# Inverting the diagonal blocks of a delta rule: two partitions to a block instead of one

## The chip and the metric

One core of one Trainium2 chip runs the whole program. The time is the device time of one launch in microseconds (us), from the first to the last instruction with the launch around it. TensorE multiplies matrices into PSUM, VectorE (DVE) and ScalarE (ACT) move and transform data, GpSimd (POOL) does elementwise work on SBUF, and SyncE (SP) issues most of the transfers. Every engine takes its instructions strictly in its own order, so one that waits holds all that stand behind it.

## The reference

The program is a stack of two small models with 256 tokens of width 1024: a gated FFN, an mLSTM mixer, a second FFN, a gated delta net, a convolutional FFN, a sliding-window attention and a last FFN. The change touches the delta net. Of its 16 heads the part that matters is this, with one lower triangular system to be solved for each chunk:

```python
m = jnp.where(strict, jnp.einsum('bnhcd,bnhsd->bnhcs', k_beta, k) * decay, 0.0)
t_mat = lax.linalg.triangular_solve(m + eye, eye, left_side=True, lower=True,
                                    unit_diagonal=True)
u = jnp.einsum('bnhcs,bnhse->bnhce', t_mat, v_beta)
...
o_i = (jnp.einsum('bhcd,bhde->bhce', qd_i, state)
       + jnp.einsum('bhcs,bhse->bhce', a_i, v_new))
```

The kernel uses chunks of 128 tokens: two chunks for each of the 16 heads, so 32 triangles of 128x128, and each has four 32x32 blocks on its diagonal: 128 blocks to invert.

## The kernel before

All projections are done by `mm3` (lines 247 to 252): a weight tile is split into a high and a low part and multiplied in three matmuls of 128x256, L250, L251 and L252. Such a triple is called a **k-step** below; eight of them make one 128-column projection. In the delta stage 44 such projections (352 k-steps, counted from the fifth projection on) are followed by the output projection `op_all` with 128 k-steps. A weight half (`raw`, eight k-steps) is loaded by SP (L163), cast by ACT to `whi` (L171) and subtracted by DVE to `wlo` (L173), some halves ahead.

Between the k-steps the delta rule itself is woven in. `Weave` keeps a clock of its own with due times for every piece and so decides, when the program is built, where each piece stands among the k-steps on TensorE; at run time the order is fixed. The pieces, for `q8` = 0 to 7 (each holds two heads and so four triangles):

- `stage1` (L930 and on) makes the triangle `u1k`; `ustore` writes it to DRAM (`ud`), and `bload` reads the 32x32 blocks back into `B`, one block on each partition.
- `invert(hf)` runs on POOL for the half `hf` (four `q8`, 64 blocks, 64 partitions): 31 steps of a product (L1016, `tmp`) and an addition (L1021, `Z`), each as long as (31-i)(i+1) elements. Then a copy makes the transpose `Y` (L1022), `X` and `Y` lying interleaved in `Z`, and one DMA writes both to DRAM (L1023, `xyd`). `INVERT_COST` tells the planner's clock how long that takes.
- `levels(q8)` reads its blocks from `xyd` into the diagonal of `XY` with four DMAs on SP's queue (L1047), after the weight load issued last, and joins the blocks to the inverse of the triangle: r32 (L1061), px32 (L1071, L1074), r64 (L1085), px64 (L1090), each followed by a copy on ACT or DVE.
- `solve` and `outp` then apply it: w1, w2, w3 (L1104, L1110, L1118), the output o (L1130 to L1132), a row norm on ACT and DVE, and transposes (L1150) with a gate, after which the head's part of `op_all` may run (mark "h").

These eight chains, called **levels** here, and the transposes of `v` (L815) are all of TensorE's work in the stage beside the k-steps. `XY` has three buffers that are cleared once by POOL at the start (L1000) and are used again; `q8` 6 and 7 take the space of `B` and `Z`, and POOL clears it (L1041, L1044).

The order of the projections is k, half of q, half of z, the rest of q and z, then the 16 of v (`GD_ORDER`). Those of v carry a convolution of three passes on DVE (L746) and a gate (L765).

Of the kernel before, what the change touches and what calls it, by code (L numbers as in the profile page):

```python
# [10 lines left out]
F32 = mybir.dt.float32  # L11
# [27 lines left out]
INVERT_COST = 51.0  # L39
# [81 lines left out]
def stack_kernel(ctx, tc, w, xt, cols, rows, gw, baw, rel, kc, kb, out):  # L121
# [582 lines left out]
    xyd = [gdr.tile([64, 32, 64], F32, name=f"xyd{i}") for i in range(2)]  # L704
# [19 lines left out]
    with tc.tile_pool(name="gd", bufs=1) as gp, tc.tile_pool(name="gw", bufs=2) as gq:  # L724
# [246 lines left out]
        def ustore(q8, j, u):  # L971
            (nc.gpsimd if q8 < 4 else nc.scalar).dma_start(out=urows(4 * q8 + 2 * j), in_=u)
            stored[0] += 1
            if stored[0] % 4 == 0 and stored[0] <= 8:
                bload(stored[0] // 4 - 1)
            if stored[0] == 16:
                yield 0.0, 4.0, 0.0
                bload(2)
                bload(3)
            if stored[0] % 8 == 0:  # L980
                fill.mark("s", stored[0] // 8 - 1)
            yield 0.0, 0.0, 0.0
# [8 lines left out]
        B = gp.tile([128, 32, 32], F32, name="B", tag="B")  # L991
        Z = gp.tile([128, 32, 32, 2], F32, name="Z", tag="Z")
        P_.memset(Z, 0.0)
        P_.memset(Z.rearrange("p a b t -> p (a b t)")[:, 0:2048:66], 1.0)
        tmp = gp.tile([128, 256], F32, name="tmp")

        lastinv = [None]
        xyt = [gp.tile([128, 4, 256], F32, name=f"XY{i}") for i in range(3)]
# [3 lines left out]
        def bload(q):  # L1002
            pr = slice(32 * q, 32 * q + 32)
            (nc.gpsimd if q < 2 else nc.scalar).dma_start(out=B[pr], in_=bass.AP(
                tensor=ud[q // 2].tensor, offset=ud[q // 2].offset + 32 * (q % 2) * 129 * 32,
                ap=[[129 * 32, 32], [128, 32], [1, 32]]))

        def invert(hf):
            p0 = 64 * hf
            pr = slice(p0, p0 + 64)  # L1010
            X, Y = Z[pr, :, :, 0], Z[pr, :, :, 1]
            first = None
            for i in range(31):
                n = 31 - i
                t = tmp[pr, 0:n * (i + 1)].rearrange("p (r j) -> p r j", r=n)
                ins = P_.tensor_tensor(out=t, in0=X[:, i, 0:i + 1].unsqueeze(1).to_broadcast([64, n, i + 1]),  # L1016
                                 in1=B[pr, i, i + 1:32].unsqueeze(2).to_broadcast([64, n, i + 1]), op=ALU.mult)
# [12 lines left out]
        def levels(q8):  # L1030
            u = [unit(), unit()]
            for j in range(2):
                nc.sync.dma_start(out=u[j], in_=urows(4 * q8 + 2 * j))
            t = max(fill.now, turn[0])
            turn[0] = t + 5.0
            yield 0.0, t - fill.now, 0.0
            if q8 < 6:
                XY = xyt[q8 % 3]
            elif q8 == 6:
                XY = gp.tile([128, 4, 256], F32, name="XY", tag="B")  # L1040
                P_.memset(XY, 0.0)  # L1041
            else:
                XY = gp.tile([128, 2048], F32, name="XY", tag="Z")[:, 0:1024].rearrange("p (g c) -> p g c", g=4)
                P_.memset(XY, 0.0)  # L1044
            src = xyd[q8 // 4]
            for a in range(4):
                ins = nc.sync.dma_start(out=XY[32 * a:32 * a + 32, :, 64 * a:64 * a + 64], in_=bass.AP(  # L1047
                    tensor=src.tensor, offset=src.offset + (16 * (q8 % 4) + a) * 2048,
                    ap=[[64, 32], [4 * 2048, 4], [1, 64]]))
                after(lastw[0], ins)  # L1050
            xyv = XY.rearrange("p g (c t) -> p g c t", t=2)
            X, Y = xyv[:, :, :, 0], xyv[:, :, :, 1]
# [12 lines left out]
            for b in (32, 96):  # L1065
                S.copy(r32[b:b + 32], pr[b:b + 32, 0:128].rearrange("p (g n) -> p g n", g=4))
# [9 lines left out]
            for b in (0, 64):  # L1076
                V.tensor_copy(Y[b:b + 32, :, b + 32:b + 64], px[b:b + 32, 0:128].rearrange("p (g n) -> p g n", g=4))
                if b == 0:
                    V.tensor_copy(X[32:64, :, 0:32], px[32:64, 0:128].rearrange("p (g n) -> p g n", g=4))
# [6 lines left out]
            S.copy(r64[64:128], pr[64:128, 0:256].rearrange("p (g n) -> p g n", g=4))  # L1086
# [388 lines left out]
```

## Time and profile before

| | us |
|---|---|
| three runs, lowest, median, highest | 1319.40, 1320.38, 1331.99 |
| the profiled execution | 1322.84 |
| its span | 1321.0 |
| TensorE busy | 1287.4 (97%) |
| DVE, ACT, POOL busy | 942.0 (71%), 787.2 (60%), 129.8 (10%) |

The span is what the trace covers; the 1.84 us around it are launch and end. All times in a trace are counted from the span's start. Matmuls overlap, so a matmul's own duration is longer than its share of the engine: the distance from one start to the next is what counts, and a TensorE busy for 97% may still run well below its rate. `PEclk` is the granted share of TensorE's full clock: 1.00 is 2.4 GHz and 0.50 is 1.2 GHz. A name such as `mm<-XY,u1k` is output, arrow, inputs. The delta stage lies between 541 and 842 us.

### The profile page before, as it was taken

What the parts mean: (1) busy time and instruction counts of PE and PEld (TensorE: products, weight loads), DVE (VectorE), ACT (ScalarE), POOL (GpSimd) and SP (SyncE); (2) the same over time, 40 slices, a digit from 0 to 9 for tenths busy, and PEclk for the clock granted to TensorE, in tenths of its full rate; (3) what the DMA queues carried; (4) which work ended last, traced back from release to release, by engine and by line L of the source; (5) the groups of instructions that cost most, each with busy time, mean ns of one, the idle gap of its engine ahead of it and who ended that gap; (6) DMA issues with size and microseconds to landing.
All of it is one profiled execution on the core that took longest, in us unless ns stands there. A gap on an engine that the chain in (4) does not pass through costs nothing.

```text
span 1321.0 us, 27393 instructions
## 1 busy us (share of the span) xinstructions
PE 1287.4 (97%) x10665; PEld 1250.2 (95%) x10665; DVE 942.0 (71%) x1856; ACT 787.2 (60%) x1823; POOL 129.8 (10%) x196
## 2 busy tenths in 40 slices
PE   9999999999999999999999899999999999999997
PEld 8999999999999999899999888899999989999997
DVE  7866546776777754588887845787886786998851
ACT  6544445665765554466666635766765676777641
POOL 0000000000000000102899200001100000000000
PEclk9999999999999999999999979999999999999998
DMA  7755553543465655226474432368976532476540
GB/s 260 242 175 176 175 176 104 170 146 95 157 201 186 190 182 172 73 92 195 127 229 146 109 124 68 128 172 222 228 219 208 178 97 78 151 236 195 190 158 33
DMA packets 72322, 213.38 MB, mean 162 GB/s; under 512 B 14597, under 2 KB 21285, under 8 KB 72064
## 3 DMA queue, kind: packets, MB, share of 16 engines
q1 hardware_dynamic: 65264, 204.36, 49.1%
q0 software_dynamic: 2240, 5.17, 1.8%
q10 hardware_dynamic: 4688, 2.10, 0.6%
q8 instruction: 84, 1.38, 0.4%
q14 instruction: 46, 0.38, 0.1%
HBM read 207.00 MB, written 4.59 MB: 160 GB/s over the span
## 4 chain that ended last, share of the span: by engine, by line
PE 74%; DVE 11%; DMA 6%; ACT 6%; issue 2%; SPq 0%; DVEq 0%; ACTq 0%
PE mm L250 11%; PE mm L251 11%; PE mm L252 11%; PE st L250 7%; PE st L251 7%; PE st L252 7%; DMA raw<-in_w 6%; DVE wlo L173 4%; ACT whi L171 2%; PE mm L270 2%; PE mm L272 2%; PE mm L268 2%; PE st L268 1%; PE st L272 1%; PE st L270 1%
## 5 line engine op out<-in xcount | busy, mean ns | idle before, releaser
L171 ACT CAST whi<-raw 128x512 fp32r<-128x512 f32 x752 | 439.3, 617 | 320.2 <-PE mm L251 112.4
L173 DVE TENSOR_TENSOR wlo<-raw,whi 128x1024 fp32r<-128x1024 f32 (+1 forms) x377 | 461.5, 1226 | 140.4 <-ACT whi L171 128.7
L250 PE MATMUL mm<-xh,whi 128*128 128x256 f32 (+1 forms) x1040 | 295.2, 284 | 0.1
L252 PE MATMUL mm<-xh,wlo 128*128 128x256 f32 (+1 forms) x1040 | 294.6, 283 | 0.0
L251 PE MATMUL mm<-xl,whi 128*128 128x256 f32 (+1 forms) x1040 | 294.2, 283 | 0.0
L250 PE MATMUL st<-xh,whi 128*128 128x256 f32 (+1 forms) x720 | 206.1, 286 | 1.1 <-DVE u1k L925 1.1
L252 PE MATMUL st<-xh,wlo 128*128 128x256 f32 (+1 forms) x720 | 204.4, 284 | 0.1
L251 PE MATMUL st<-xl,whi 128*128 128x256 f32 (+1 forms) x720 | 204.3, 284 | 0.0
L252 PEld LDWEIGHTS mm<-xh,wlo 128*128 128x128 f32 x1040 | 196.0, 188 | 0.5 <-DVE wlo L173 0.2
L250 PEld LDWEIGHTS mm<-xh,whi 128*128 128x128 f32 x1040 | 196.0, 189 | 0.5 <-DVE fu L428 0.3
L251 PEld LDWEIGHTS mm<-xl,whi 128*128 128x128 f32 x1040 | 195.8, 188 | 0.7 <-DVE xl L380 0.6
L250 PEld LDWEIGHTS st<-xh,whi 128*128 128x128 f32 x720 | 136.1, 189 | 2.6 <-DVE u1k L925 1.3
L252 PEld LDWEIGHTS st<-xh,wlo 128*128 128x128 f32 x720 | 136.2, 189 | 0.5 <-DVE wlo L173 0.5
L251 PEld LDWEIGHTS st<-xl,whi 128*128 128x128 f32 x720 | 135.9, 189 | 0.0
L250 PE MATMUL mm<-hh,whi 128*128 128x256 f32 (+1 forms) x352 | 99.5, 283 | 0.0
L251 PE MATMUL mm<-hl,whi 128*128 128x256 f32 (+1 forms) x352 | 99.4, 282 | 0.0
L252 PE MATMUL mm<-hh,wlo 128*128 128x256 f32 (+1 forms) x352 | 99.4, 282 | 0.0
L250 PEld LDWEIGHTS mm<-hh,whi 128*128 128x128 f32 x352 | 67.0, 190 | 0.0
L251 PEld LDWEIGHTS mm<-hl,whi 128*128 128x128 f32 x352 | 66.5, 189 | 0.0
L252 PEld LDWEIGHTS mm<-hh,wlo 128*128 128x128 f32 x352 | 66.5, 189 | 0.0
L439 DVE SCALAR_TENSOR_TENSOR fu<-mm,colt,fu 128x255 f32<-128x255 f32 x108 | 51.1, 477 | 14.0 <-ACT fu L436 13.8
L250 PE MATMUL st<-hh,whi 128*128 128x256 f32 (+1 forms) x176 | 49.7, 282 | 0.0
(489 smaller groups left out, 2696.5 us busy)
## 6 DMA issues: line engine op xcount, KB each, us to landing
raw<-in_w SPq DMA_DIRECT2D x377, 512.0 KB, 4.3
u1k<-ud SPq DMA_DIRECT2D x16, 128.0 KB, 5.5
Tb<-bvd POOLq DMA_DIRECT2D x16, 128.0 KB, 5.7
gx<-in_w SPq DMA_DIRECT2D x2, 512.0 KB, 5.6
ud<-u1k POOLq DMA_DIRECT2D x8, 128.0 KB, 2.9
ud<-u1k ACTq DMA_DIRECT2D x8, 128.0 KB, 2.6
xyd<-Z POOLq DMA_DIRECT2D x2, 512.0 KB, 4.5
XY<-xyd SPq DMA_DIRECT2D x32, 32.0 KB, 2.1
```

What stands on the lines that cost most here:

```text
L171: S.copy(hi[:, c[0]:c[1]], raw[:, c[0]:c[1]])
L173: V.tensor_tensor(out=lo[:, c[0]:c[1]], in0=raw[:, c[0]:c[1]], in1=hi[:, c[0]:c[1]].bitcast(F32), op=ALU.subtract)
L250: T_.matmul(ps, hi, xhh, start=first, stop=False)
L251: T_.matmul(ps, hi, xll, start=False, stop=False)
L252: lastmm[0] = T_.matmul(ps, lo, xhh, start=False, stop=last)
L268: T_.matmul(pss[j], wts[j][0], xhh, start=(k == 0), stop=False)
L270: T_.matmul(pss[j], wts[j][1], xhh, start=False, stop=False)
L272: T_.matmul(pss[j], wts[j][0], xll, start=False, stop=(k == kt - 1))
L439: V.scalar_tensor_tensor(out=t[:, d:], in0=ps[:, :T - d], scalar=wc(2 - d), in1=t[:, d:], op0=ALU.mult, op1=ALU.add)
```

## The change

Each block now has two partitions: partition 64 `par` + n holds the columns of parity `par` (even, odd) of block n. So one call of `invert` uses 128 partitions, and step i works on (31-i)(i//2+1) elements. `X` and `Y` lie one after the other in `Z`, sixteen columns each. `B` is loaded twice, once for each parity (`bload`, now together after the eighth store of a half; half of the loads go on ACT's queue), and there are a `B` and a `Z` for each half. `xyd` is written by two DMAs. The pieces are put in order by `levels`: X columns land as "even columns first" by six DMAs, Y rows by eight DMAs into every second partition, 14 for a `q8` instead of 4, and the copies from PSUM permute columns where the two orders meet. `XY` has two cleared buffers; `q8` 2 to 5 take the space of B0, Z0, B1 and Z1 and are cleared by DVE (2 and 3) or POOL (4 and 5). `INVERT_COST` is 34.0 instead of 51.0.

```diff
-INVERT_COST = 51.0
+INVERT_COST = 34.0
...
-    xyd = [gdr.tile([64, 32, 64], F32, name=f"xyd{i}") for i in range(2)]
+    xyd = [gdr.tile([2, 64, 2, 512], F32, name=f"xyd{i}") for i in range(2)]
...
-            if stored[0] % 4 == 0 and stored[0] <= 8:
-                bload(stored[0] // 4 - 1)
-            if stored[0] == 16:
+            if stored[0] % 8 == 0:
+                hf = stored[0] // 8 - 1
                 yield 0.0, 4.0, 0.0
-                bload(2)
-                bload(3)
-            if stored[0] % 8 == 0:
-                fill.mark("s", stored[0] // 8 - 1)
+                bload(2 * hf)
+                bload(2 * hf + 1)
+                fill.mark("s", hf)
...
         def bload(q):
-            pr = slice(32 * q, 32 * q + 32)
-            (nc.gpsimd if q < 2 else nc.scalar).dma_start(out=B[pr], in_=bass.AP(
+            for par in range(2):
+                p0 = 64 * par + 32 * (q % 2)
+                (nc.gpsimd if q < 2 and par == 0 else nc.scalar).dma_start(out=Bs[q // 2][p0:p0 + 32], in_=bass.AP(
...
             for i in range(31):
-                n = 31 - i
+                n, w = 31 - i, i // 2 + 1
...
-                P_.tensor_tensor(out=X[:, i + 1:32, 0:i + 1], in0=X[:, i + 1:32, 0:i + 1], in1=t, op=ALU.add)
-            lastinv[0] = P_.tensor_copy(Y, X.rearrange("p i j -> p j i"))
-            nc.gpsimd.dma_start(out=xyd[hf], in_=Z[pr].rearrange("p a b t -> p a (b t)"))
+                P_.tensor_tensor(out=X[:, i + 1:32, 0:w], in0=X[:, i + 1:32, 0:w], in1=t, op=ALU.add)
+            lastinv[0] = P_.tensor_copy(Y, X.rearrange("p i c -> p c i"))
+            for par in range(2):
+                nc.gpsimd.dma_start(out=xyd[hf][par], in_=z[64 * par:64 * par + 64].rearrange("p (t e) -> p t e", t=2))
...
-            if q8 < 6:
-                XY = xyt[q8 % 3]
...
+            if q8 in (0, 1, 6, 7):
+                XY = xyt[q8 % 2]
             else:
...
+                XY = gp.tile([128, 2, 4, 128], F32, name="XY", tag=("B0", "Z0", "B1", "Z1")[q8 - 2])
+                (V if q8 < 4 else P_).memset(XY, 0.0)
...
             for a in range(4):
-                ins = nc.sync.dma_start(out=XY[32 * a:32 * a + 32, :, 64 * a:64 * a + 64], in_=bass.AP(
...
+                r0 = 32 * a
+                for par in range(2):
+                    c0 = r0 + 16 * par
+                    if a < 3:
+                        ins = nc.sync.dma_start(out=XY[r0:r0 + 32, 0, :, c0:c0 + 16],
+                                                in_=part(par, a, 0, [[16, 32], [4 * 1024, 4], [1, 16]]))
+                        after(lastw[0], ins)
+                    ins = nc.sync.dma_start(out=XY[r0 + par:r0 + 32:2, 1, :, r0:r0 + 32],
+                                            in_=part(par, a, 1, [[32, 16], [4 * 1024, 4], [1, 32]]))
+                    after(lastw[0], ins)
...
-            if 3 <= q8 < 6:
+            if q8 >= 6:
                 cond.append(("h", q8 - 3))
```

The planner's new numbers move the pieces. Counted in the order of TensorE, with the 480 k-steps of the stage as a ruler, the first r32 stood at k-step 305 and now stands at 270. The o of `q8` 0, 1 and 2 stood before k-step 352, the end of the projections; now those of 0 to 3 do, and those of 4 and 5 follow at 353. The last four transposes (L1150, now L1160) stood at 464 and now stand at 433. How that looks on TensorE at the last chain: before, all four transposes stand together, and behind them the k-steps of the last heads begin in four accumulators at once.

```order
L250 MATMUL ax<-u1k,whi 128x256
L251 MATMUL ax<-u1k,whi 128x256
L252 MATMUL ax<-u1k,wlo 128x256
L1150 MATMUL mm<-kct,u1k 128x128 x4
L250 MATMUL st<-u1k,whi 128x256 x2
L250 MATMUL ax<-u1k,whi 128x256 x2
L251 MATMUL st<-u1k,whi 128x256
L252 MATMUL st<-u1k,wlo 128x256
```

Now, on the same engine and for the same chain, 31 k-steps earlier, each transpose stands between matmuls that read earlier heads:

```order
L250 MATMUL st<-u1k,whi 128x256
L1160 MATMUL mm<-kct,u1k 128x128
L251 MATMUL st<-u1k,whi 128x256
L1160 MATMUL mm<-kct,u1k 128x128
L252 MATMUL st<-u1k,wlo 128x256
L1160 MATMUL mm<-kct,u1k 128x128
```

The last k-steps no longer stand right behind the transposes that they need.

On DVE, in the z projections, two clearings have come in ahead of gates of z (L925) and weight splits (L173); the rows marked + are new. The first writes the space of B0, the second that of Z0.

```order
 L925 SCALAR_TENSOR_TENSOR u1k<-zt,st 128x256
 L173 TENSOR_TENSOR wlo<-raw,whi 128x1024 x2
+L1043 MEMSET XY 128x1024
 L925 SCALAR_TENSOR_TENSOR u1k<-zt,st 128x256
 L925 SCALAR_TENSOR_TENSOR u1k<-zt,ax 128x256
 L173 TENSOR_TENSOR wlo<-raw,whi 128x1024
+L1043 MEMSET XY 128x1024
 L925 SCALAR_TENSOR_TENSOR u1k<-zt,st 128x256
```

So DVE cannot pass the first before POOL has read B0 for the last time, nor the second before `xyd` of the first half has left Z0.

On SP's queue, before, the reads of both halves (`xyd_4357` is the first, `xyd_4358` the second) stand late among the weight loads:

```order
L163 DMA raw<-in_w 128x1024
L1047 DMA XY_6826<-xyd_4357 32x4x64 x4
L163 DMA raw<-in_w 128x1024 x6
L1047 DMA XY_6824<-xyd_4357 32x4x64 x4
L1047 DMA XY_6825<-xyd_4358 32x4x64 x4
L163 DMA raw<-in_w 128x1024
```

Now the second half's first read stands eight weight loads earlier, and the 28 reads of `q8` 4 and 5 stand together; this is their end:

```order
L1053 DMA XY<-xyd_4358 32x4x16
L1056 DMA XY<-xyd_4358 16x4x32 x3
L1038 DMA u1k<-ud_4356 128x2x128 x2
L163 DMA raw<-in_w 128x1024 x2
L1053 DMA XY_6830<-xyd_4358 32x4x16
```

The weight loads behind the 28 reads wait with them for the second half's `xyd`.

## Rows read from the trace of the kernel before

**Rows 1.** Stretches: us, busy us by engine, PEclk, DMA share, GB/s
```profile
core 0: us, PE busy (x) PEld busy (x) DVE busy (x) ACT busy (x) POOL busy (x), PEclk, DMA share, GB/s
674.90:745.30 70.40, 64.80 (x614) 61.06 (x613) 58.88 (x128) 46.57 (x140) 56.34 (x77) 0.98 0.47 138
745.30:842.00 96.70, 90.99 (x815) 82.06 (x814) 53.99 (x163) 49.32 (x154) 0.00 (x0) 0.91 0.36 114
740.20:743.60 3.40, 3.40 (x19) 3.40 (x18) 2.12 (x5) 2.12 (x12) 0.95 (x1) 0.50 0.16 34
777.70:791.40 13.70, 13.40 (x111) 12.01 (x111) 3.34 (x10) 4.43 (x12) 0.00 (x0) 0.50 0.10 38
835.80:839.20 3.40, 3.40 (x18) 3.40 (x18) 0.65 (x2) 0.40 (x1) 0.00 (x0) 0.50 0.49 154
```

**Rows 2.** Timeline of TensorE: start us, us, engine, line, operation
```profile
674.53 0.28 PE L250 MATMUL st<-xh,whi 128*128 128x256 f32 x1
...
675.95 0.28 PE L250 MATMUL st<-xh,whi 128*128 128x256 f32 x1
...
703.58 0.59 PE L1061 MATMUL mm<-XY,u1k 32*32 32x32 f32 x16
704.10 0.39 PE L250 MATMUL st<-xh,whi 128*128 128x256 f32 x1
...
723.98 0.49 PE L1130 MATMUL mm<-u1k 128*128 128x128 f32 x2
...
725.42 0.28 PE L1110 MATMUL mm<-u1k 128*128 128x128 f32 x1
```

**Rows 3.** Waits of TensorE, 674.9 to 842: total us, times, longest
```profile
PE mm L1150 <- ACT u1k L1146: 5.0, 3, 2.7
PE ax L815 <- DVE gy L765: 2.9, 5, 1.3
PE st L250 <- ACT u1k L390: 1.3, 2, 1.0
```

**Rows 4.** Timeline of POOL, first pass and the start of the second
```profile
629.14 0.23 POOL L1016 TENSOR_TENSOR tmp<-Z,B 64x31 f32<-64x31 f32 x1 [2.76 <-DMA B<-ud]
629.45 0.26 POOL L1021 TENSOR_TENSOR Z<-Z,tmp 64x31 f32<-64x31 f32 x1
...
655.45 0.73 POOL L1021 TENSOR_TENSOR Z<-Z,tmp 64x252 f32<-64x252 f32 x1
656.26 1.48 POOL L1016 TENSOR_TENSOR tmp<-Z,B 64x247 f32<-64x247 f32 x1
...
680.52 2.90 POOL L1022 COPY Z<-Z 64x1024 f32<-64x1024 f32 x1
683.71 0.58 POOL L1023 DMA_DIRECT2D xyd<-Z  x1 [0.30 <-DMA raw<-in_w]
684.36 0.24 POOL L1016 TENSOR_TENSOR tmp<-Z,B 64x31 f32<-64x31 f32 x1
```

**Rows 5.** Groups by line, POOL and DVE: busy us, mean ns, idle before
```profile
L1379 POOL TENSOR_TENSOR o<-o,rb 128x256 f32<-128x256 f32 x2 | 1.4, 721 | 346.4 <-ACT rb L363 346.4
L229 DVE MEMSET ones<- 128x128 f32 x1 | 0.2, 165 | 0.8 <-PEq L1463 0.8
L231 DVE MEMSET epsc<- 128x1 f32 x1 | 0.1, 59 | 0.0
```

**Rows 6.** Timeline of DVE where the clearings come in
```profile
662.16 2.89 DVE L173 TENSOR_TENSOR wlo<-raw,whi 128x1024 fp32r<-128x1024 f32 x2
665.63 1.21 DVE L173 TENSOR_TENSOR wlo<-raw,whi 128x1024 fp32r<-128x1024 f32 x1
667.33 0.42 DVE L925 SCALAR_TENSOR_TENSOR u1k<-zt,st 128x256 f32<-128x256 f32 x1 [0.49 <-ACT zt L923]
```

**Rows 7.** Timeline of SP's queue
```profile
681.61 0.35 SPq L163 DMA_DIRECT2D raw<-in_w  x1
688.53 1.75 SPq L1047 DMA_DIRECT2D XY<-xyd  x4
...
723.47 19.62 SPq L1047 DMA_DIRECT2D XY<-xyd  x8
```

**Rows 8.** Issues of DMAs, whole span: KB each, us to landing
```profile
xyd<-Z POOLq DMA_DIRECT2D x2, 512.0 KB, 4.5
XY<-xyd SPq DMA_DIRECT2D x32, 32.0 KB, 2.1
```

More of the change, by code (lines that the diff above doesn't have):

```diff
@@ L989, in front @@
             fill.mark("f", hf)
[L991 to L995, printed above, removed]
+        Bs = [gp.tile([128, 32, 32], F32, name=f"B{i}", tag=f"B{i}") for i in range(2)]
+        Zs = [gp.tile([128, 1024], F32, name=f"Z{i}", tag=f"Z{i}") for i in range(2)]
+        for z in Zs:
+            P_.memset(z, 0.0)
+            for par in range(2):
+                P_.memset(z[64 * par:64 * par + 64, 16 * par:512:33], 1.0)
+        tmp = gp.tile([128, 144], F32, name="tmp")
         lastinv = [None]
-        xyt = [gp.tile([128, 4, 256], F32, name=f"XY{i}") for i in range(3)]
+        xyt = [gp.tile([128, 2, 4, 128], F32, name=f"XY{i}") for i in range(2)]
         for t in xyt:
@@ L1030, in levels @@
         def levels(q8):
+            t = max(fill.now, turn[0])
+            turn[0] = t + 5.0
+            yield 0.0, t - fill.now, 0.0
             u = [unit(), unit()]
@@ L1033, in levels, with part @@
                 nc.sync.dma_start(out=u[j], in_=urows(4 * q8 + 2 * j))
-            t = max(fill.now, turn[0])
-            turn[0] = t + 5.0
-            yield 0.0, t - fill.now, 0.0
-            if q8 < 6:
-                XY = xyt[q8 % 3]
-            elif q8 == 6:
-                XY = gp.tile([128, 4, 256], F32, name="XY", tag="B")
-                P_.memset(XY, 0.0)
-            else:
-                XY = gp.tile([128, 2048], F32, name="XY", tag="Z")[:, 0:1024].rearrange("p (g c) -> p g c", g=4)
-                P_.memset(XY, 0.0)
+            if q8 in (0, 1, 6, 7):
+                XY = xyt[q8 % 2]
+            else:
+                XY = gp.tile([128, 2, 4, 128], F32, name="XY", tag=("B0", "Z0", "B1", "Z1")[q8 - 2])
+                (V if q8 < 4 else P_).memset(XY, 0.0)
             src = xyd[q8 // 4]
+            def part(par, a, t, ap):
+                return bass.AP(tensor=src.tensor, offset=src.offset + (par * 64 + 16 * (q8 % 4) + a) * 1024 + t * 512, ap=ap)
             for a in range(4):
-                ins = nc.sync.dma_start(out=XY[32 * a:32 * a + 32, :, 64 * a:64 * a + 64], in_=bass.AP(
[L1048 to L1052, printed above, removed]
+                r0 = 32 * a
+                for par in range(2):
+                    c0 = r0 + 16 * par
[6 more added lines that the diff above has]
+                    after(lastw[0], ins)
+            X, Y = XY[:, 0], XY[:, 1]
             yield 0.0, 3.0, 0.0
@@ L1065, in levels @@
             for b in (32, 96):
-                S.copy(r32[b:b + 32], pr[b:b + 32, 0:128].rearrange("p (g n) -> p g n", g=4))
+                S.copy(r32[b:b + 32].rearrange("p g (c t) -> p g c t", t=2),
+                       pr[b:b + 32, 0:128].rearrange("p (g t c) -> p g c t", g=4, t=2))
             yield 0.5, 0.9, 0.0
@@ L1078, in levels @@
                 if b == 0:
-                    V.tensor_copy(X[32:64, :, 0:32], px[32:64, 0:128].rearrange("p (g n) -> p g n", g=4))
+                    V.tensor_copy(X[32:64, :, 0:32].rearrange("p g (t c) -> p g c t", t=2),
+                                  px[32:64, 0:128].rearrange("p (g c t) -> p g c t", g=4, t=2))
             yield 1.0, 0.4, 0.8
@@ L1085, in levels @@
                 T_.matmul(pr[64:128, g * 64:g * 64 + 64], us(g, 0, 64, 64, 64), X[0:64, g, 0:64], start=True, stop=True)
-            S.copy(r64[64:128], pr[64:128, 0:256].rearrange("p (g n) -> p g n", g=4))
+            S.copy(r64[64:128].rearrange("p g (b c t) -> p (g b) c t", b=2, t=2),
+                   pr[64:128, 0:256].rearrange("p (g b t c) -> p (g b) c t", g=4, b=2, t=2))
             yield 0.43, 0.7, 0.0
```

16 lines of the change are left out of this document (8 added, 8 removed).

## Prediction

> **What bounds the kernel now.** I read the stretches of the delta stage first, then TensorE's own timeline, its waits, and at last POOL, DVE and SP, whose order the change alters. TensorE is the engine to look at: outside this stage nothing changes, and the stage ends when its last k-step does. The question is how much of the stage TensorE needs, and how much it loses.
>
> The stretch from 674.9 to 745.3 us holds k-steps 240 to 352, the projections of v; that from 745.3 to 842.0 holds the 128 k-steps of the output projection [rows 1]. Four k-steps start 1.42 us apart, 0.355 us each [rows 2]. An r32 takes 0.52 us, from 703.58 to the next start at 704.10; the six pieces of an o take 1.44, 0.24 each [rows 2]. I put px32, r64 and px64 at 0.6 each, like r32, w1 to w3 at two such pieces each (1.44 together) and the transposes at 0.45: 5.6 us for a level. A transpose pair of v I put at 0.3.
>
> - Stretch of v: 112 x 0.355 = 39.8, three levels (those of `q8` 0 to 2) 16.8, 14 pairs 4.2: 60.8 us of work in 70.4. Of the 9.6 lost, 1.7 are the 3.4 us at half clock [rows 1], 2.9 are waits of the pairs for DVE [rows 3], and 5.0 remain: 1.7 for each level.
> - Tail: 128 x 0.355 = 45.4 and five levels 28.0: 73.4 us of work in 96.7. Of the 23.3 lost, 8.5 are the 17.1 us at half clock [rows 1], and 14.8 remain: 3.0 for each level.
>
> The losses of a level are waits for the copies between its steps; the longest are the transposes' for ACT's normed rows and the output projection's for its first operands [rows 3]. In the tail five levels share 128 k-steps, and those of head k/2 may not start before that head's level has ended. The clock fell to 1.2 GHz there, in 13.7 us of which ACT and DVE were also nearly idle [rows 1].
>
> **The change, part by part.**
>
> *POOL's pass.* A pass has 62 operations. 31 elements took 0.23 us [rows 4], and 256 took 0.72 on 128 partitions [rows 5]: 2.2 ns for an element and 0.16 fixed, with 0.08 between operations [rows 4]. The 128 partitions cost nothing by that row. The sum of (31-i)(i//2+1) is 2856, used twice: 62 x 0.24 + 5712 x 0.0022 = 27.4 us. To that come stalls: 247 elements took 1.48 us where 252 took 0.73 [rows 4]; 24 of the 124 operations are such, about one in 4.2 us, at 0.75 to 0.9. Eight or nine of them make 35 us, against 51.4 from 629.14 to 680.5 [rows 4]. Bounds: 27.4 with no stall, 39 with as many stalls for each operation as now. The start stays: each `B` load still follows the same store, and the second parity's goes on ACT's queue beside it.
>
> So the first pass ends at 664. The copy has half the elements, 1.5 for 2.9 us [rows 4], two issues of 0.58 follow, and the landing takes at most the 4.5 us of the larger store [rows 8]: the first `xyd` is there at 671.5, not 688.2. The second pass ends at 702.5 and its `xyd` is there at 710.
>
> *SP's queue.* A read of `xyd` took 0.44 us to issue (1.75 for four) and 2.1 to land [rows 7, 8]. Fourteen take 6.1 us, so the first r32 has its data at about 680. TensorE reaches it 30 k-steps and four pairs of v past 674.9, at 687 to 689: hidden by 7 us. All 80 added issues are 35 us of SP. The pieces are shorter: runs of 64 and 128 bytes. The Trainium skill (DMA: Bandwidth & Descriptors, Specifications) wants at least 512 bytes in a transfer for the full rate and speaks against them; the reads now are 256 bytes long, already under it, and land in 2.1 us [rows 8]. By the rule shorter runs would land later; if the time doubled (an estimate, the page has no figure), the first r32 would still be hidden, and the sum stays.
>
> What is not free are the weight loads behind the reads. The 28 reads of `q8` 4 and 5 can start at 710 and take 12.3 us, so the two weight loads behind them leave at 722, some 20 us after the two before. SP has stood so long before, 19.62 us on eight reads [rows 7], and TensorE waited for no weight then [rows 3]. I take 1 us; the ends are nothing and 4 us (the issue to landing of a load, if the lead is used up).
>
> *DVE's clearings.* One is about 0.9 us (59 ns for one element, 165 for 128) [rows 5]. The first stands behind the split that ends at 665.05 [rows 6], POOL is done at 664: no wait. The second stands ahead of the gate at 667.33 [rows 6] and must wait for the landing at 671.5: 4.2 us, and with both clearings DVE is 6 us late. Behind it stand gates of z, which free TensorE's accumulators, weight splits, and then the convolutions of v. TensorE writes into other accumulators meanwhile, but DVE is busy 58.9 of 70.4 us afterwards [rows 1] and makes the time up slowly. I take 2.5 us on the path; the ends are nothing and 6.
>
> *The levels move.* Nearly six levels (5.7) now have their work in the stretch of v, 2.3 in the tail. A level there costs 1.7 of loss in the one stretch and 3.0 in the other, by the rows above. The stretch of v gets fuller: DVE and ACT must do the copies of 2.7 more levels beside the convolutions, so 1.7 is too little; 3.0, where the output projection was held up by heads not ready, is too much. I take 2.0. In the tail I keep 3.0. No head is late for the output projection by the new order, since the last transposes stand 31 k-steps earlier, and the long stretch at half clock should go; I leave one short one, 1.7 us.
>
> The sum: stretch of v 39.8 + 31.9 + 4.2 work, 2.9 + 11.4 + 2.5 + 1.0 lost: 93.7 us. Tail 45.4 + 12.9 work, 6.9 + 1.7 lost: 66.9. Together 160.6 against 167.1: **6.5 us less**. The work is the same to the last matmul; only losses change. From the profiled execution's 1322.84 that gives 1316.3. The median of the runs shown is 2.5 lower, so I predict 1314.
>
> **The rivals.**
>
> *The levels hide fully.* With a k-step always free to run, a level may lose only what TensorE's listed waits for ACT make, 6.3 us for eight [rows 3], 0.8 each. That saves another 5.7 x 1.2 + 2.3 x 2.2 = 11.9: 1302. For it: the waits listed are few. Against it: the tail's 3.0, which is far more than its listed waits.
>
> *The losses only move.* The levels of `q8` 2 to 5 stand close together now, with few k-steps between; that is what the tail looked like ahead of the stretch at half clock. If the clock is lost as long as now, 6.8 us of the gain go, and if DVE's whole 6 us arrive, 3.5 more: 1324. For it: TensorE's work in the stretch is short matmuls; against it: what followed the tail's waits were heads not ready, and those are gone.
>
> *The pass is not halved,* and the kernel is slower. If an operation on 128 partitions took twice as long as on 64, the first `xyd` would land at 688 as now, but DVE stands for it from 667.3: 16.8 us more than above, of which the accumulators and weights ahead hide about 5. The second `xyd` would be at 740, the weight loads behind the reads at 752 instead of 722, past the lead that hid 20 us: some 13 us. 1314 + 12 + 13 = 1339. It decides from a first landing past about 676; each further us is lost in full. Against it stands the one row of 128 partitions [rows 5].
>
> **How the numbers follow.** The forecast, 1307 to 1320, gets 0.53; full hiding 0.22; losses that only move 0.20; no halving 0.05. A measurement of this kernel can tell about 1% from no change, 13 us. Faster by more than that is most of the second case and the forecast's lower edge, 0.24; slower is the fourth, 0.05; between lie 0.71. The range goes from 1301, with full hiding in it, to 1325, with losses that only move in it; the unknown prices (clearing 0 to 6, weights 0 to 4, a level 0.8 to 3.0) stay within that. Outside are no halving and the edges, under 2 in 10.
>
> **What would show it.** Right: POOL's first pass 33 to 38 us and both `xyd` stores landed before 675 and 715; a wait of 3 to 5 us of DVE's second clearing for `xyd`; the first r32 near 688 without a wait for a DMA; k-step 352 reached some 20 us later than 745, and the end of the stage 5 to 8 us earlier than 842; at most one short stretch of PEclk 0.50. Wrong: a pass over 42 us; DVE idle for 10 us at the clearing; TensorE waiting for `wlo` or `whi` near the reads of `q8` 4 and 5; a long stretch at half clock; or a stretch of v under 85 us, which would mean full hiding.

## The result, and the profile after

The changed kernel takes 1330.41 us (median of 20 runs, 1324.37 to 1334.19), beside 1321.19 us for the kernel before (20 runs): a ratio of **1.0055, 95% interval [1.0039, 1.0071]**. By the ratio that is 7 us slower (9 between the two medians) where 6.5 us less was forecast, and above the range that ended at 1325; the difference is under 1%.

The profiled execution took 1325.46 us (span 1323.6), one of the shorter ones. It is only 2.6 us above the profiled one of before, because the part behind the stage, which is the same program, took 476.0 us in it and 479.0 in that of before. The stage itself is 305.3 us long (542.3 to 847.6), before 300.2: there the loss is seen.

Stretches of the changed kernel; the bounds are k-steps 120, 149, 188, 240, 352 and the end of the stage, and then the stretches at half clock. Columns as in [rows 1]. Pieces of levels stand among the matmuls of the last two k-steps of v until 788, so the bound at 782 is good to about 1 us.

```profile
core 0: us, PE busy (x) PEld busy (x) DVE busy (x) ACT busy (x) POOL busy (x), PEclk, DMA share, GB/s
618.60:637.90 19.30, 16.07 (x105) 15.24 (x104) 11.90 (x26) 9.02 (x23) 7.85 (x16) 0.82 0.44 127
...
660.20:684.60 24.40, 21.40 (x161) 20.98 (x160) 15.54 (x29) 11.62 (x28) 14.90 (x26) 0.89 0.69 193
684.60:782.00 97.40, 89.02 (x870) 80.30 (x870) 67.78 (x180) 58.37 (x179) 30.95 (x61) 0.92 0.41 112
782.00:847.60 65.60, 63.86 (x557) 60.16 (x556) 39.40 (x110) 38.81 (x115) 0.00 (x0) 1.00 0.45 142
624.40:631.30 6.90, 6.12 (x28) 6.13 (x29) 4.05 (x10) 0.98 (x3) 1.47 (x2) 0.51 0.52 135
679.00:685.90 6.90, 5.95 (x28) 5.95 (x29) 5.46 (x8) 1.56 (x4) 5.29 (x10) 0.51 0.46 137
757.60:761.00 3.40, 3.40 (x17) 3.40 (x18) 2.48 (x7) 1.51 (x6) 0.00 (x0) 0.50 0.32 79
767.80:778.00 10.20, 10.20 (x80) 9.23 (x78) 6.25 (x11) 6.36 (x15) 0.00 (x0) 0.50 0.30 66
```

The same k-steps in the kernel before, 120 to 149 and 188 to 240:

```profile
620.10:633.10 13.00, 11.41 (x93) 10.96 (x92) 10.13 (x23) 7.85 (x19) 5.63 (x11) 1.00 0.53 155
...
656.10:674.90 18.80, 18.80 (x162) 18.80 (x161) 16.06 (x28) 11.46 (x27) 17.39 (x19) 1.00 0.74 221
```

Against [rows 1] the stretch of v grew from 70.4 to 97.4 us and the tail shrank from 96.7 to 65.6, together 4.1 us less, as the forecast had it in kind. But k-step 240 is reached 9.7 us later, at 684.6 instead of 674.9: 4.8 us are lost by k-step 149 and 5.6 more between 188 and 240. In both places TensorE first stands and then runs 6.9 us at half clock. At the first, the pieces of stage1 (L933 to L947) now stand together with no k-step among them; the changed kernel, then the one before:

```profile
620.22 0.38 PE L947 MATMUL mm<-kct,gc 128*128 128x128 f32 x2
621.57 0.43 PE L947 MATMUL mm<-kct,gc 128*128 128x128 f32 x2 [0.98 <-ACT dc L952]
623.17 0.70 PE L933 MATMUL mm<-u1k 128*128 128x256 f32 x2 [1.16 <-ACT dc L952]
...
625.17 0.58 PE L250 MATMUL st<-xh,whi 128*128 128x256 f32 x1 [1.08 <-DVE u1k L925]
```

```profile
621.08 0.70 PE L933 MATMUL mm<-u1k 128*128 128x256 f32 x2 [0.50 <-ACT dc L952]
...
623.09 0.39 PE L250 MATMUL st<-xh,whi 128*128 128x256 f32 x1 [1.09 <-DVE u1k L925]
```

POOL, from the first pass to the second store (start us, us, engine, line, operation, wait before it):

```profile
632.03 0.23 POOL L1017 TENSOR_TENSOR tmp<-Z,B 128x31 f32<-128x31 f32 x1 [4.04 <-DMA B<-ud]
...
669.88 1.09 POOL L1023 COPY Z<-Z 128x512 f32<-128x512 f32 x1
671.27 1.13 POOL L1025 DMA_DIRECT2D xyd<-Z  x2 [0.29 <-POOL Z L1023]
679.90 1.22 POOL L1017 TENSOR_TENSOR tmp<-Z,B 128x31 f32<-128x31 f32 x1 [7.50 <-DMA B<-ud]
...
718.20 1.10 POOL L1025 DMA_DIRECT2D xyd<-Z  x2 [0.29 <-POOL Z L1023]
724.07 0.94 POOL L1043 MEMSET XY<- 128x1024 f32 x1 [4.77 <-DMA xyd<-Z]
```

The pass is shorter, 37.8 us (632.0 to 669.8) instead of 51.4 [rows 4]. Its two stores have landed 7.4 us after the first issue, at 678.7, where DVE has been waiting for it and TensorE for DVE. First DVE at its two clearings, then TensorE:

```profile
669.80 0.91 DVE L1043 MEMSET XY<- 128x1024 f32 x1 [2.07 <-POOL tmp L1017]
...
678.71 0.91 DVE L1043 MEMSET XY<- 128x1024 f32 x1 [6.26 <-DMA xyd<-Z]
679.54 0.36 DVE L925 SCALAR_TENSOR_TENSOR u1k<-zt,st 128x256 f32<-128x256 f32 x1
```

```profile
676.67 0.28 PE L252 MATMUL ax<-xh,wlo 128*128 128x256 f32 x1
679.95 0.58 PE L250 MATMUL st<-xh,whi 128*128 128x256 f32 x1 [3.00 <-DVE u1k L925]
```

The gate L925 behind the clearing frees TensorE's accumulator; the next k-step starts 3.28 us after the one before it. From 683.5 on SP is the busy one. Its queue while the reads of the first `q8` go out:

```profile
681.05 1.84 SPq L163 DMA_DIRECT2D raw<-in_w  x2
683.00 0.38 SPq L1038 DMA_DIRECT2D u1k<-ud  x1
683.48 0.41 SPq L1053 DMA_DIRECT2D XY<-xyd  x1
683.94 0.69 SPq L1056 DMA_DIRECT2D XY<-xyd  x1
...
690.64 1.84 SPq L1056 DMA_DIRECT2D XY<-xyd  x3
692.58 1.00 SPq L163 DMA_DIRECT2D raw<-in_w  x2
...
748.36 0.89 SPq L163 DMA_DIRECT2D raw<-in_w  x2
```

Fourteen reads take 9.0 us (683.48 to 692.48), 0.64 each instead of 0.44 [rows 7], and the reads go on with few pauses until 776: only 11 weight halves leave in between. TensorE then meets weights that become ready in the moment in which it wants them:

```profile
735.66 0.28 PE L251 MATMUL st<-xl,whi 128*128 128x256 f32 x1
737.02 0.39 PE L252 MATMUL st<-xh,wlo 128*128 128x256 f32 x1 [1.08 <-DVE wlo L173]
...
755.24 0.28 PE L251 MATMUL st<-xl,whi 128*128 128x256 f32 x1
757.07 0.39 PE L250 MATMUL st<-xh,whi 128*128 128x256 f32 x1 [1.55 <-ACT whi L171]
```

So there were three suspects, and a fourth question: (A) DVE's clearings; (C) the moved loads of `B`, with the reordered stage1 at k-step 120; (D) SP's 112 reads; and (E) whether the earlier levels are worth anything. All ratios below are to the kernel before, with 95% intervals, and a part is one in 1000; two ratios can be told apart from about 2 to 4 parts on, depending on their intervals. Two of the runs below had one execution each at a low clock (2073.7 us at 0.56 in the run with the later clearings, 1394.8 at 0.84 in the first with seven reads), which the ratios leave out.

### The profile page after: what moved, and what is told of

Read it like the earlier page. It is cut to its first block, busy times and chain, and to the rows that moved or that the text cites. A ratio compares the mean times of both kernels' runs of the same rounds, so it can differ in the third digit from the quotient of the medians.

```text
span 1323.6 us, 27500 instructions
## 1 busy us (share of the span) xinstructions
PE 1288.2 (97%) x10665; PEld 1251.9 (95%) x10665; DVE 934.1 (71%) x1858; ACT 788.5 (60%) x1823; POOL 101.9 (8%) x201
## 4 chain that ended last, share of the span: by engine, by line
PE 82%; DVE 6%; ACT 4%; DMA 3%; POOL 3%; issue 2%; SPq 0%; DVEq 0%; ACTq 0%; POOLq 0%
PE mm L250 12%; PE mm L252 12%; PE mm L251 12%; PE st L250 8%; PE st L252 8%; PE st L251 7%; DVE wlo L173 2%; PE mm L270 2%; PE mm L272 2%; PE mm L268 2%; POOL Z L1022 1%; POOL tmp L1017 1%; ACT whi L171 1%; PE st L268 1%; PE st L272 1%
## 5 line engine op out<-in xcount | busy, mean ns | idle before, releaser
L173 DVE TENSOR_TENSOR wlo<-raw,whi 128x1024 fp32r<-128x1024 f32 (+1 forms) x377 | 459.3, 1220 | 144.5 <-ACT whi L171 138.0
L250 PE MATMUL st<-xh,whi 128*128 128x256 f32 (+1 forms) x720 | 209.1, 290 | 5.6 <-DVE u1k L925 4.1
L252 PE MATMUL st<-xh,wlo 128*128 128x256 f32 (+1 forms) x720 | 207.3, 288 | 1.4 <-DVE wlo L173 1.3
L251 PE MATMUL st<-xl,whi 128*128 128x256 f32 (+1 forms) x720 | 207.1, 288 | 0.0
L250 PEld LDWEIGHTS st<-xh,whi 128*128 128x128 f32 x720 | 139.4, 194 | 7.6 <-DVE u1k L925 4.5
L252 PEld LDWEIGHTS st<-xh,wlo 128*128 128x128 f32 x720 | 139.0, 193 | 2.2 <-DVE wlo L173 2.0
L251 PEld LDWEIGHTS st<-xl,whi 128*128 128x128 f32 x720 | 139.0, 193 | 0.1
```

The source lines that it names most:

```text
L173: V.tensor_tensor(out=lo[:, c[0]:c[1]], in0=raw[:, c[0]:c[1]], in1=hi[:, c[0]:c[1]].bitcast(F32), op=ALU.subtract)
L250: T_.matmul(ps, hi, xhh, start=first, stop=False)
L251: T_.matmul(ps, hi, xll, start=False, stop=False)
L252: lastmm[0] = T_.matmul(ps, lo, xhh, start=False, stop=last)
```

## The experiments

### The order alone: levels back at their old place

```diff
-INVERT_COST = 34.0
+INVERT_COST = 51.0
```

> The changed kernel with INVERT_COST 51.0 as before: POOL's pass stays 38 us, but the planner puts the levels where they stood before the change, 32 k-steps later. Theory E (the earlier order costs: crowded levels at a stage where weights, reads and copies collide): the stretch from k-step 240 to the end loses what the early order lost, and the time falls by 3 us or more, to 1.002 or below, although no level is hidden better. Rival F (the order is right and the stalls ahead of it cost): the tail's half clock comes back (13.7 us at half clock before) and the time is the same or up to 5 us longer, 1.005 to 1.009.

Measured: 1339.72 us, **1.0130 [1.0102, 1.0158]**. The earlier levels are not the loss: with the order made for 51.0 it is 7.5 parts worse. The tail then took 107 us (750.5 to 857.5).

### One cause at a time: clearings, loads of B, number of reads

```diff
-                (V if q8 < 4 else P_).memset(XY, 0.0)
+                ins = (V if q8 < 4 else P_).memset(XY, 0.0)
+                if q8 < 4:
+                    after(splits[-4], ins)
```

(`splits` holds the instructions of L173 so far.)

> The changed kernel, with DVE's two clearings of XY (q8 2 and 3) ordered behind the fourth-last weight split, so that they stand some 15 us later on DVE, after the first xyd has landed; nothing else. Theory A (the clearing is what costs): DVE no longer stands 6.3 us for xyd, TensorE's gap of 3.3 us at 676.7 and the half clock behind it (6.8 us, 3.4 lost) go, k-step 240 is reached 5 to 7 us earlier, and the time falls by 5 to 7 us, to about 1324 or a ratio of 1.000 to before. Rival B (the waits only move; the time is set by the crowded levels behind it): k-step 240 earlier, but the time within 2 us of the changed kernel, 1.004 to 1.006.

Measured: 1326.03 us, **1.0033 [1.0015, 1.0051]**. DVE no longer waits, the gap at 676.7 and the half clock behind it are gone, and k-step 240 comes at 677.8, 6.8 us earlier; 1.5 us of that were won by k-step 149, where the stretch at half clock was only 3.4 us long in this execution. The time fell by 2.2 parts, 3 us, at the edge of what can be told apart. In the profiled executions 3.3 us were lost again behind k-step 240.

```diff
-            if stored[0] % 8 == 0:
-                hf = stored[0] // 8 - 1
+            if stored[0] % 4 == 0 and stored[0] <= 8:
+                bload(stored[0] // 4 - 1)
+            if stored[0] == 16:
                 yield 0.0, 4.0, 0.0
...
+            if stored[0] % 8 == 0:
+                fill.mark("s", stored[0] // 8 - 1)
...
-                (nc.gpsimd if q < 2 and par == 0 else nc.scalar).dma_start(
+                (nc.gpsimd if q < 2 else nc.scalar).dma_start(
```

> The changed kernel, with the loads of B for the first half issued as before, after the fourth and the eighth store and both parities on POOL's queue, and the mark 's' set without a delay; the second half's loads stay together on ACT's queue. The order of the first 240 k-steps on TensorE then is that of the kernel before. Theory C (the reordered stage1 costs): the four gaps between 620 and 625 us and the half clock of 6.8 us behind them go, k-step 149 is reached 4 us earlier, the time falls by 3 to 5 us, ratio about 1.002. POOL's first pass starts near 629, not 632. Rival: the two parities' loads one after another on POOL start the pass no earlier, and the time stays at 1.005.

Measured: 1323.61 us, **1.0017 [0.9988, 1.0047]**. K-step 149 is at 633.5, as before the change; the half clock there is gone. POOL's pass starts only 1.7 us earlier, at 630.3: the loss up to there was TensorE's order more than POOL's start. The edit undoes three things at once, the queue of half the loads, the planner's delay ahead of them and the place of the mark "s"; which of them moves stage1 was not taken apart.

```diff
+                nc.gpsimd.dma_start(
+                    out=bass.AP(tensor=d.tensor, offset=d.offset + par * 16, ap=[[2048, 64], [32, 32], [1, 16]]),
...
+                nc.gpsimd.dma_start(
+                    out=bass.AP(tensor=d.tensor, offset=d.offset + 1024 + par * 32, ap=[[2048, 64], [64, 16], [1, 32]]),
...
+                for t in range(2) if a < 3 else (1,):
+                    ins = nc.sync.dma_start(out=XY[r0:r0 + 32, t, :, r0:r0 + 32], in_=bass.AP(
+                        tensor=src.tensor, offset=src.offset + (16 * (q8 % 4) + a) * 2048 + t * 1024,
+                        ap=[[32, 32], [4 * 2048, 4], [1, 32]]))
```

> The changed kernel, with the parities brought together by the stores (four stores for a half, with runs of 64 and 128 bytes in DRAM) so that a q8 needs seven reads instead of 14; the copies from PSUM are as in the changed kernel. Theory D (SP's reads cost): SP stands 4 us instead of 8 to 10 for a q8, the weight splits behind the reads come earlier, the waits of TensorE for whi, wlo and XY between 735 and 770 us (some 6 us) shrink, and the time falls by 3 to 5 us, ratio about 1.002. Rival: SP's reads are hidden by the weights ahead and the time stays within 2 us of the changed kernel; or the scattered stores land later than 7 us after their issue and DVE's second clearing stands longer by as much, ratio 1.007 or more.

Measured: 1324.32 us, **1.0010 [0.9991, 1.0028]**, 4.5 parts less than the changed kernel, although both stalls ahead of k-step 240 stayed and the second grew (k-step 240 at 687.0).

### All combinations of the three

> The two mends of the stalls ahead of k-step 240 together: DVE's clearings ordered behind the fourth-last weight split, and the first half's loads of B on POOL after the fourth and the eighth store. One theory, that the two losses are separate and each is lost in full (4.4 us by k-step 149 and 5.4 us from 188 to 240): k-step 240 is reached near 673.5 us and the time falls by the sum of the two single runs, 2.2 + 3.8 parts in 1000, to a ratio of 0.9995. The rival, that the levels behind take back what is gained ahead because SP, DVE and the copies hold them up: ratio 1.001 to 1.003, no better than the better of the two.

> The same with seven reads for a q8 instead of 14 and four scattered stores for a half. If SP's issue time of the reads is what holds the levels and the weights behind them from k-step 271 on, the gain of that single run (4.5 parts in 1000) comes on top: ratio 0.995. If the reads only mattered because the clearings and B were late: the ratio of the two mends, within 0.002.

> The changed kernel with seven reads and with DVE's clearings later; B's loads as in the changed kernel. If the three mends add up only when SP is free: between the seven reads alone (1.001) and all three (0.993), at about 0.996, since k-step 240 is reached some 9 us earlier than with seven reads alone, where DVE stood 5 us longer. If the loads of B were what counted beside the reads: 1.000 to 1.001.

> The changed kernel with seven reads and with the first half's loads of B as before; DVE's clearings as in the changed kernel. If the clearing's stall is lost in full: 4 us less than with seven reads alone, 0.998, and worse than with the later clearings. If the loads of B count as much as the clearings: 0.995 to 0.996.

| reads for a q8 | clearings and B as changed | clearings later | B as before | both |
|---|---|---|---|---|
| 14 | 1.0055 | 1.0033 | 1.0017 | 1.0025 [0.9993, 1.0058] |
| 7 | 1.0010 | 0.9989 [0.9970, 1.0009] | 0.9964 [0.9945, 0.9982] | **0.9928 [0.9903, 0.9953]** |

The two mends are the later clearings and the loads of `B` as before; seven reads are the third. With 14 reads the two mends together came out no better than one of them; the 0.9995 that their sum would give lies just inside the interval, so by the times alone this is not shown. With seven they add: 2.1 and 4.6 parts alone, 8.2 together. The profiles say more. With both mends k-step 240 is back where it was before the change, 133 us behind the stage's start (142 in the changed kernel). From there to the end it then took 173.4 us with 14 reads, 10 more than in the changed kernel (in an execution 4 us above the median), and 155.5 with seven. So what the mends gain ahead of k-step 240 was kept only where the stretch behind it could take it. Each of these runs also has an order of its own behind k-step 240. The kernel with all three, 1311.41 us, beats both kernels. Its stage from k-step 240 on, and its stretch at half clock:

```profile
674.40:757.40 83.00, 76.51 (x783) 70.83 (x782) 65.62 (x173) 54.36 (x169) 34.52 (x69) 0.98 0.53 148
757.40:829.90 72.50, 71.05 (x650) 65.54 (x649) 44.04 (x121) 42.15 (x127) 0.00 (x0) 1.00 0.37 121
680.70:684.10 3.40, 3.31 (x16) 3.32 (x17) 3.24 (x7) 0.93 (x3) 3.01 (x6) 0.50 0.48 121
```

All of TensorE's waits between 670 and 852 us in it:

```profile
PE ax L816 <- DVE gy L766: 3.0, 1, 3.0
PE mm L1120 <- ACT u1k L1121: 2.7, 1, 2.7
PE mm L1166 <- ACT u1k L1162: 1.9, 3, 0.8
PE st L253 <- DVE wlo L173: 0.2, 1, 0.2
```

From k-step 240 to the end it needs 155.5 us, where before needed 167.1 [rows 1] and the changed kernel 163.0. Weights are waited for 0.2 us.

The order again, now with the stalls mended:

> The kernel with all three mends, and INVERT_COST 51.0, so that the levels stand where they stood before the change. If the gain of the three-mend kernel (0.993) is the earlier levels: about the time before or more, 1.000 to 1.005, with a stretch at half clock in the tail. If it is only the mended stalls: 0.993 again.

Measured: **1.0017 [0.9994, 1.0040]**. With the order made for 51.0 nothing is left of the gain: the order with earlier levels is worth 8.9 parts (12 us) with the three mends, and 7.5 (10 us) in the changed kernel.

### Loads of B off ACT's queue

ACT stood 4.7 us on the fourth load of the second half's `B` (669.33 to 674.0; the three before took 0.33 to 0.50 us), and POOL's second pass waited 7.5 us for it. Edit: `q >= 2 and par == 1` go to `nc.gpsimd`, in the changed kernel and in the one with three mends.

> The changed kernel, with only the second half's loads of B for odd columns moved from ACT's queue to POOL's. Theory: ACT's 4.7 us on the fourth issue (669.3 to 674.0) delay casts of weights and gates and add to TensorE's gap at 676.7, and the second pass starts 7.5 us late: 2 to 3 us less, ratio 1.003. Rival: DVE, which stands until 678.7 at the clearing anyway, covers both, and the time is that of the changed kernel, 1.005.

> The same with the second half's loads of B for odd columns on POOL's queue, so that ACT issues two instead of four of them. ACT no longer stands 4.7 us on the fourth issue, and POOL's second pass starts some 3 us earlier. If the second xyd is what the levels of q8 4 to 7 wait for: 2 to 4 us less than the kernel with three mends, 0.992 to 0.994. If not, the same within 0.002.

Measured: **1.0108 [1.0085, 1.0131]** and **0.9984 [0.9959, 1.0010]**, both about 5 parts worse. ACT's stand was gone, but the second pass began no earlier (679.5) in the one and 7 us later in the other (681.6 instead of 674.5), since POOL can issue its load only behind its first pass. That this is the whole of the 5 parts is not shown: the order moved too.

### SP's queue, or the order?

```diff
-                    ins = nc.sync.dma_start(out=XY[r0 + par:r0 + 32:2, 1, ...
-                    after(lastw[0], ins)
+                    ins = (nc.sync if q8 < 4 else nc.gpsimd).dma_start(out=XY[r0 + par:r0 + 32:2, 1, ...
+                    if q8 < 4:
+                        after(lastw[0], ins)
```

> The changed kernel, with the eight reads of Y for each of q8 4 to 7 on POOL's queue, where nothing else stands after the second pass; the same 14 reads of the same size, SP issues 32 fewer. Theory (SP's queue is what holds the second half of the levels and the weights among them: it issues reads without a pause from 683 to 776 us): TensorE's waits for whi, wlo and XY between 735 and 767 us shrink, k-step 352 comes 5 to 10 us earlier, and the time falls by 3 to 6 us, ratio 1.001 to 1.003. Rival (it is the size of the transfers, not who issues them): the reads land as late, ratio 1.004 to 1.007.

Measured: 1320.32 us, **0.9966 [0.9945, 0.9987]**: 8.9 parts less than the changed kernel, by 32 reads of the same size on another queue. K-step 352 came at 758.8 instead of 782, but that is not all time won, since the order changed: between k-steps 320 and 352 it has 78 matmuls of levels and of v where the changed kernel has 286. The profiled stage is 10.7 us shorter: 2.8 of these were won up to 744 us, as long as TensorE, DVE and ACT have the same order in both, and 7.9 behind that, where the orders differ. SP gained more than the 32 issues. The reads of `q8` 4 to 7 that are left on it are those of X, and six in a row took 0.47 us each:

```profile
735.72 2.82 SPq L1053 DMA_DIRECT2D XY<-xyd  x6
```

In the changed kernel the same reads stand between those of Y, and a pair of the two takes about 1.2 us.

> The changed kernel with 14 reads of the same size, the reads of Y for q8 4 to 7 on POOL's queue, and the two mends ahead of k-step 240 (later clearings, B's loads as before). With all reads on SP these two mends gave 1.0025, no more than one of them alone. If it was SP's queue that took their gain back: they now add to 0.9966, and the ratio is 0.990 to 0.993. If they never add, whatever SP does: 0.995 to 0.998.

> The kernel with three mends (seven reads, 0.9928), with the four reads of Y for q8 4 to 7 on POOL's queue besides. If SP is still the bound in the second half of the levels: another 2 to 5 us, 0.989 to 0.991. If seven reads already free it: 0.992 to 0.994.

Measured: **0.9954 [0.9933, 0.9975]** and **0.9921 [0.9892, 0.9949]**. With seven reads no gain can be told any more. With 14, the mends add 1.2 parts, which is within the noise: between k-steps 240 and 308 this kernel has 322 matmuls of levels and of v where the run without the mends has 180, and it ran 10.2 us at half clock there (from 723.9). The order had moved again. So the next run kept it: TensorE, DVE and ACT were chained, instruction by instruction, in the order of the kernel compared with.

```diff
+        for engine, text in ORDER.items():
+            at = in_order(text)
+            for x, y in zip(at, at[1:]):
+                after(seen[engine][x], seen[engine][y])
```

> As the run that moved 32 reads of Y from SP to POOL (0.9966), but with every instruction on TensorE, DVE and ACT kept in the order of the changed kernel; in that run the planner's order behind k-step 312 had changed too. Only who issues 32 reads differs from the changed kernel. If it is SP's queue that costs: ratio 0.996 to 0.999, and the weight halves no longer become ready in the moment in which TensorE wants them (737.0 and 757.5 us). If the gain came from the other order: 1.004 to 1.007, as the changed kernel.

Measured: 1332.24 us, **1.0070 [1.0046, 1.0094]**. **In the changed kernel's order a freer SP brings nothing.** Late reads do not explain that: on POOL's queue they landed after 4.4 us (2.0 in the changed kernel), but TensorE waits for none of them. The same weight half shows why. Its load on SP and its cast on ACT in the changed kernel:

```profile
748.36 0.89 SPq L163 DMA_DIRECT2D raw<-in_w  x2
```

```profile
753.26 1.16 ACT L1156 ACTIVATE u1k<-mm,rq_y 128x128 f32<-128x128 f32 x4
754.26 1.19 ACT L171 CAST whi<-raw 128x512 fp32r<-128x512 f32 x2
```

in this run (its operations bear the line of the helper that records them), with TensorE:

```profile
736.44 0.85 SPq L219 DMA_DIRECT2D raw<-in_w  x2
```

```profile
755.21 1.16 ACT L95 ACTIVATE u1k<-mm,rq_y 128x128 f32<-128x128 f32 x4
756.21 1.19 ACT L95 CAST whi<-raw 128x512 fp32r<-128x512 f32 x2
```

```profile
757.19 0.28 PE L95 MATMUL st<-xl,whi 128*128 128x256 f32 x1
759.02 0.58 PE L95 MATMUL st<-xh,whi 128*128 128x256 f32 x1 [1.55 <-ACT whi L95]
```

and in the run where the order could follow:

```profile
734.80 0.86 SPq L163 DMA_DIRECT2D raw<-in_w  x2
```

```profile
743.18 1.13 ACT L171 CAST whi<-raw 128x512 fp32r<-128x512 f32 x2
```

The load leaves 12 us earlier in the kept order (whose stage began 1.8 us later), but its cast stands behind the norms of a level (L1156), which wait for TensorE, and TensorE waits the same 1.55 us for it. Where the order was made anew for the freer queue, the cast stands 11 us earlier. With the same reads on POOL the two orders are 10.4 parts apart, so the order is where the time is. That the changed kernel's was made for a queue full of reads is how I read it, since the one edit on the queue brought the other order. The new order with all reads on SP was not run; in the changed kernel this half's load left SP only at 748.36, behind the place (743.18) that the new order gives its cast, so a freer queue is probably needed too.

> The changed kernel with seven reads and four scattered stores, as in the run that gave 1.001, but with TensorE, DVE and ACT kept in the order of the changed kernel. If SP's queue is the bound: 0.995 to 0.999, less than with seven reads alone, where the levels of q8 0 to 2 had moved closer together ahead of k-step 312. If order and queue count alike: about 1.001 again.

Measured: 1340.68 us, **1.0149 [1.0111, 1.0186]**: seven reads in an order made for 14 are worse still. DVE's second clearing, which waits for their four stores, stood 9.0 us instead of 6.26, SP waited 12.8 us for the second `xyd`, and TensorE 5.4 us for loads of `ud` behind it. The trace also has 47.8 us at half clock in the stage (27.4 in the changed kernel), and how the 9.4 parts divide stays open.

> The kernel before, with ten more reads for each q8 on SP's queue (32 partitions with runs of 64 bytes, into a spare tile that nothing reads), between the four that it has; TensorE, DVE and ACT keep the order of the kernel before in the stage. All else is as before: pass on 64 partitions, levels late, clearings on POOL. By the forecast (SP's 80 added issues are hidden, 1 us for the weights behind them): 1.000 to 1.002. By the theory that SP's queue is the bound once 14 reads stand for each q8: 5 to 12 us more, 1.004 to 1.009.

```diff
+                for e in range(3 if a < 2 else 2):
+                    ins = nc.sync.dma_start(out=spare[32 * a:32 * a + 32, e], ...)
```

(64-byte runs of `xyd`, into a tile that nothing reads.)

Measured: 1346.56 us, **1.0182 [1.0145, 1.0219]**. Ten more reads for each `q8` cost the kernel before 24 us, in its own order. They go out at about 0.47 us each, so 80 make 38 us of SP. Not all of the cost is issue time: reads of the second half came to stand ahead of weight loads, and SP waited 18.0 us with them for the second `xyd`. How much is the one and how much the other stays open.

## Why the prediction was wrong

Two steps failed. The sum took the way to k-step 240 as unchanged, and it was reached 9.7 us later. And it took SP's reads as hidden, where they went along with an order that cost 12 us. Behind k-step 240 the sum itself came out near, 163.0 us for 160.6, but partly by luck, since two misses cancel in part: its 2.5 us for the clearing fell ahead of k-step 240, and two stretches at half clock lost up to 6.8 us behind it where 1.7 were allowed.

- **POOL's pass**: forecast 35 us within 27.4 to 39, measured 37.8, with nine operations of 1.15 to 1.43 us among its 62, the forecast's eight or nine stalls. Right. **"The start stays"**: wrong. It came 2.9 us later. POOL still issues its loads behind the fourth and the eighth store, as before the change (616.45 and 627.20); but the eighth store left 2.1 us later (624.36, before 622.27), behind the stage1 that had moved, and from the last load to the pass it took 4.8 us instead of 3.6. With 37.8 and a landing of 7.4 instead of 4.5 us, `xyd` was there at 678.7, not 671.5. The second `xyd`, forecast at 710, came at 724: the second pass stood 7.5 us for its last load of `B`.
- **What was left out**: this is the first failed step, a term put at nothing without a reason. The edit of the loads, their delay and the mark "s" also moved stage1 on TensorE (no k-step stands among its matmuls now, from 618.9 to 625.2), and 4.8 us went by k-step 149, half clock included. Undoing it gave 3.8 parts (5 us).
- **DVE's clearing**: the mechanism was named, a wait for `xyd` with the gate behind it. 4.2 us of wait were forecast, 6.26 measured, and 2.07 at the first clearing where none was expected. On the path 2.5 us were taken; between k-steps 188 and 240 it was 5.6, more than half of it the clock (6.9 us at half clock, 3.4 lost); in the whole time the later clearing gave 3 us.
- **SP's queue**: the second failed step. "Hidden by 7 us", and 1 us for the weights. The first r32 was indeed hidden (its reads were out at 692.5, TensorE came at 698.6). But a read took 0.64 us, 112 of them filled the queue until 776, and with the order that went with that, 32 reads on SP instead of on POOL cost 8.9 parts, 12 us; with the order kept, the same 32 reads made no difference that can be told (1.0070 beside 1.0055). I had weighed the reads as a delay of data in a given order. What costs is the order: a weight cast stands 11 us later in it, and 286 matmuls of levels and of v are crowded between k-steps 320 and 352, where the other order has 78. Of the signs of being wrong that the prediction named, TensorE's waits for `wlo` and `whi` came, 1.08 and 1.55 us.
- **Short runs**: the reads landed after 2.0 us, before 2.1 [rows 8], but at 8 KB each instead of 32. By the Trainium skill (DMA: Bandwidth & Descriptors, Specifications) transfers under 512 bytes lose rate; no later landing shows here at 64 and 128 bytes, and no run measures the rate. What grew is the issue time, and not by the length of the runs: reads of X with 64-byte runs took 0.47 us each in a row, and 0.6 between those of Y.
- **Levels**: the tail was forecast at 66.9 us and took 65.6; the stretch of v 93.7, and took 97.4. One short stretch at half clock was left in the sum, 1.7 us lost; in the whole stage there were four, 27.4 us long, up to 13.7 us lost (20.5 us and 10.2 in the kernel before). The gain of the order is real, 10 to 12 us by the two runs with 51.0, more than the 6.5 forecast. The levels also need not move that far: the kernels with seven reads or with reads on POOL, each in an order of its own made for 34.0, have 374 to 432 matmuls of levels and of v between k-steps 240 and 352 and ratios of 1.0010 and less; the changed kernel has 582, the one before 276. That the number itself is the cause is not shown.
- **The rivals**: "the losses only move" came nearest, with DVE's whole wait and a lost clock; it gave 1324. "No halving" is out, by the 37.8 us: the kernel is slower, as that rival had it, but not for its reason. Full hiding (1302) did not come either: with the stalls mended and seven reads, 1311.4.

## What to carry to other kernels

A faster step moves everything that was timed around it: look at what comes to wait for its result (here a clearing on DVE ahead of the gates), and at the queue that fetches it. Count the DMAs that a layout needs, not only their bytes, and put parts together where they are stored once rather than where they are read many times. Where the order is made when the program is built, an edit on one queue can change the order of all engines, so it must be tried with the order made anew, and also with it kept. And look at the clock behind each stall: here each of two stalls of about 3 us was followed by 6.9 us at half clock, and the loss was about twice the stall.

## What was not expected of the hardware

- In the changed kernel a read of `xyd` into every second of 32 partitions (Y, 64 runs of 128 bytes) held SP 0.56 us, and one into 32 partitions (X, 128 runs of 64 bytes) 0.58 where it stood behind one of Y. Six of X in a row, with 32 reads of Y moved to POOL, took 2.82 us, 0.47 each; 128 runs of 256 bytes took 0.44 [rows 7]. So neither the number nor the length of the runs explains the 0.56; why the reads of Y take longer is open.
- The fourth of the second half's loads of `B` held ACT for 4.7 us (4.3 in the kernel with three mends), the three before it 0.33 to 0.50.
- Two stores of 256 KB issued one after the other released the waiting DVE 7.4 us after the first issue, and the second pair POOL after 5.9; the one of 512 KB before took 4.5 [rows 8].
